# Opening of a gated recurrent and pooling layer: warm-up on a constant, one input piece cast in two parts, two sums held back in the plan

## The chip, the cores and the metric

The kernel runs on one core of a Trainium2 chip. The metric is the device time of one execution in microseconds (us), as the median of several runs. The engines are named as in the profile: PE (TensorE, matmul) with PEld (its weight loads), DVE (VectorE), ACT (ScalarE), POOL (GpSimd) and SP (the engine that issues most DMAs).

## The reference

One layer over 1024 positions of width 1024, in float32, cut to what matters:

```python
h = jnp.einsum('bsd,de->bse', x, w_in[l]) + b_in[l]
xa, za, xb, zb, ga, gb = jnp.split(h, splits, axis=-1)
xa = _causal_depthwise_conv(xa, conv_w[l], conv_b[l])
ya = _rg_lru(xa, w_rgate[l], b_rgate[l], w_igate[l], b_igate[l], lru_lambda[l]) * jax.nn.silu(za)
yb = _multiscale_pool(xb, w_pool[l], b_pool[l], pool_scale[l]) * jax.nn.silu(zb)
merged = (jax.nn.sigmoid(ga) * jnp.einsum('bsw,wd->bsd', ya, w_proj_a[l])
          + jax.nn.sigmoid(gb) * jnp.einsum('bsw,wd->bsd', yb, w_proj_b[l]))
y = jnp.einsum('bsd,de->bse', merged, w_out[l]) + b_out[l]
x = _layer_norm(DEEPNORM_ALPHA * x + y, ln_gain[l], ln_bias[l])
```

The change lies in the first microseconds of the first product, `x @ w_in`. Its 6144 output columns are worked through as 24 groups: `G` groups are the gates `ga` and `gb`, `A` groups the pairs `xa`/`za`, `B` groups the pairs `xb`/`zb`.

## The kernel before, in words

**Products.** A float32 product is made of three matmuls in a narrower float type: each operand is split into a high part (a cast on ACT, names ending in `h`) and a low part (the rest, a subtraction on DVE, names ending in `l`); the products high·high, low·high and high·low are added in PSUM. Each large product is cut into 2x2 blocks and done with seven block products instead of eight, on sums of blocks. One block product is 12 matmuls of 128x512 (four quarters `q` of the contraction, three passes each).

**The input.** `x` arrives transposed as eight raw tiles `xr`, two for each quarter. Its blocks become `x13h/x13l` (two blocks side by side), `x` and `xb` (high and low part in one tile), the differences `t` (made by `sum57`, later `sum6` and `sum4`), and from `t` the tiles `x57h/x57l` and `x64h/x64l`. The first 256 or 512 columns of a tile can be cast by themselves, `PARTS` being the two halves of 512 columns.

**The opening.** `WARM` matmuls on a zeroed tile `warm` run first, into `ps_warm`. Then the first gate group is done without block sums: 96 block passes into `ps_s`, in the order of the quarters, each quarter in the order (kh, h) = (0,0), (1,1), (0,1), (1,0), for both weight blocks `w0h/w0l`. In the first quarter the piece (0,0) is cast and multiplied in two column parts, the others whole.

**What follows.** Group `A0` takes its seven products as `a_A`, `e_A`, `f_A` (product 5), `c_A` (product 7), again `f_A` (product 3); then the next gate group begins with `a_G` and `e_G`, then `a_A` (product 6 of `A0`), `c_G`, `a_G` and so on. Its weights come as raw tiles `ra_G` and `rb_G`; `wah_G/wal_G` is the split of `ra_G`; the split `wd_G` of half of `rb_G` is followed by three block sums in `rb_G` and `ra_G` on DVE, and from these come `wbh_G/wbl_G` (used by `c_G`) and `wch_G/wcl_G` (used by `a_G`). A finished product that is needed later is copied out of PSUM by ACT (`copied`: `m_A<-f_A` is such a copy).

**What sets the order.** The code does not issue instructions: it records them as tasks in a `Plan`. PE and POOL keep the order of the code. For ACT, DVE and SP a list scheduler (`Plan.order`) walks through estimated times, and among the tasks that it takes to be ready it starts the one with the earliest due time; due times are counted back from PE's estimated times. What comes out is written once, in a fixed order for each engine: on the chip each engine works through its list strictly, and an instruction whose input is late holds up everything behind it. All recorded instructions have one line in the profile, the `emit` helper's L388, so they are told apart by tile names.

Of the kernel before, what the change touches and what calls it, by code (L numbers as in the profile page):

```python
# [11 lines left out]
F32 = mybir.dt.float32  # L12
F32R = mybir.dt.float32r
# [3 lines left out]
P = 128  # L17
# [3 lines left out]
H = 512  # L21
# [2 lines left out]
EPS = 1e-5  # L24
WINDOWS = (2, 4, 8, 16)
PAD = 16
WARM = 6
NW = 10
NR = 4
NWORK = 10  # L30
# [24 lines left out]
class Ref:  # L55


    def __init__(self, tile_, v, chain=()):
        self.tile, self.v, self.chain = tile_, v, chain
# [96 lines left out]

class Task:
    __slots__ = ("i", "eng", "op", "args", "kw", "outs", "ins", "deps", "users", "time", "wait", "table", "due",
                 "start", "end", "left", "ready", "chain", "dma", "new", "late")


class Plan:
# [4 lines left out]

    def __init__(self, tc):
        self.tc, self.tasks, self.chained, self.last, self.late = tc, [], [set()], {}, LATEST
        for name, eng in (("tensor", "PE"), ("vector", "DVE"), ("scalar", "ACT"), ("gpsimd", "POOL"), ("sync", "SP")):  # L170
            setattr(self, name, Engine(self, name, eng))

    @contextmanager
    def within(self, us):
        self.late, late = us, self.late
        yield
        self.late = late

    def add(self, name, eng, op, args, kw):
        t = Task()  # L180
        t.late = self.late
        t.i, t.eng, t.op, t.args, t.kw = len(self.tasks), eng, (name, op), args, kw
        refs = [a for a in list(args) + list(kw.values()) if isinstance(a, Ref)]
        out = args[0]
        t.outs = [out] if isinstance(out, Ref) else []
        t.ins = refs[1:] if t.outs else refs
        if isinstance(kw.get("accum_out"), Ref):
            t.ins = [r for r in t.ins if r is not kw["accum_out"]]
            t.outs.append(kw["accum_out"])
        t.deps, t.users, t.new = set(), [], []  # L190
        add = kw.get("accum_op") is not None or (op == "matmul" and not kw.get("start"))
        for refs, write in ((t.ins, False), (t.outs, True)):
            for r in refs:
                s = r.tile
                if t.i not in s.users[-1:]:
                    s.users.append(t.i)
                a0, a1, b = g = r.region()
                for old in ((s.writes, s.reads) if write else (s.writes,)):
                    for (c0, c1, d), j in old:
                        if j != t.i and c0 <= a1 and a0 <= c1 and d & b:  # L200
                            t.deps.add(j)
                if write:

                    for old in (s.writes, s.reads):
                        old[:] = [x for x in old if not (a0 <= x[0][0] and x[0][1] <= a1 and x[0][2] & b == x[0][2])]
                (s.writes if write else s.reads).append((g, t.i))
                if write and s.tag and not s.pool.dram:
                    t.new.append(s)
        t.chain = self.last.get(eng) if eng in ("PE", "POOL") or any(eng in c for c in self.chained) else None
        self.last[eng] = t.i  # L210
        self.cost(t, add)
        self.tasks.append(t)

    def cost(self, t, add):

        name, op = t.op
# [35 lines left out]
    def order(self):  # L252
# [15 lines left out]
                t.due = min(t.due, T[u].due - t.wait)  # L268
        tags = {}
        for t in T:  # L270
            t.left, t.ready, t.start = len(t.deps), 0.0, None
            for s in t.new:
                if s.left == 0:
                    s.left = len(s.users)
                    tags.setdefault(s.tag, ([0.0] * s.pool.bufs, []))[1].append(s)
# [51 lines left out]
        while done < len(T):  # L327
            moved = True
            while moved:
                moved = False  # L330
                while state["pe"] < len(pe) and pe[state["pe"]].left == 0:
                    t = pe[state["pe"]]
# [7 lines left out]
                for e in ("ACT", "DVE", "SP", "POOL"):  # L340
# [17 lines left out]
                    for t in sorted(can, key=key):  # L358
                        end = now + t.time + (1.29 if t.table and state["table"] not in t.table else 0.0)
# [41 lines left out]
def layer_kernel(ctx: ExitStack, tc: tile.TileContext, xq, x, w_in, par, wg, w_pool, wpa, wpb, w_out, rows, out):  # L401
    nc = Plan(tc)
# [24 lines left out]
    def kt(name, dt=F32):  # L427
        return kpool.tile([P, S], dt, tag="k", name=name)

    def et(name):  # L430
        return epool.tile([P, H], F32, tag="e", name=name)

    def bank(name):
        return psum.tile([P, H], F32, tag="ps", name=name)
# [6 lines left out]
    V, A = nc.vector, nc.scalar  # L441
# [171 lines left out]
    def load_group(i, w=None, todo=("12", "4", "75", "63")):  # L613
        w = w or weights_steps(i)
        for js in ("4", "75", "63 apart", "12") if i >= len(order) - 2 else todo:
            w.step(js)
        return w.out
# [332 lines left out]


    begin = ctx.enter_context(ExitStack())
    pass
    warm = kt("warm", F32R)[:, :H]
    V.memset(warm.bitcast(F32), 0.0)
    psw = bank("ps_warm")
    for i in range(WARM):
        nc.tensor.matmul(psw, warm[:, 0:P], warm, start=True, stop=True)
# [16 lines left out]
    def split_w0(n, a, b, h=slice(0, 2)):  # L975
        split(*(w0_part(t, n, a, b)[:, h] for t in (wr, wh, wl)))
# [13 lines left out]
    def split_x(q, kh, h, sl=slice(0, H)):  # L990
        i, p = raws[kh, h]
        split(xr[q][i][:, HALF[p]][:, sl], *(t[:, sl] for t in quarter(q, kh, h)))
# [3 lines left out]
    def mm0(q, kh, h, n, cs=slice(0, H)):  # L996
        sl = slice(q * P, (q + 1) * P)
        passes(ps0[n][h][:, cs], (wh[n][:, kh, sl], wl[n][:, kh, sl]), tuple(t[:, cs] for t in quarter(q, kh, h)),
               q == 0 and kh == h and cs.start == 0, q == KQ - 1 and kh != h)


    PARTS = [slice(0, H // 2), slice(H // 2, H)]
# [63 lines left out]
    def parts(q, n=0):  # L1066
        r = xr[q][0].rearrange("p (i s) -> p i s", i=2)
        todo = [(r, *x13[q])] + [(xr[q][raws[p][0]][:, HALF[raws[p][1]]], *quarter(q, *p)) for p in ((0, 1), (1, 0))]
        for raw, t, u in todo[n:]:
            hi(raw, t)  # L1070
        for raw, t, u in todo[n:]:
            lo(raw, t, u)
        for kh, h in ((0, 0), (1, 1), (0, 1), (1, 0)):
            for n in range(2):
                mm0(q, kh, h, n)

    def each(f, qs, *a):
        for q in qs:
            f(q, *a)

    split_w0(0, 0, 1, slice(0, 1))
    for kh, h in ((0, 0), (1, 1), (0, 1), (1, 0)):
        if kh == h == 1:
            split_w0(0, 0, 1, slice(1, 2))
        for sl in PARTS if kh == h == 0 else (slice(0, H),):
            split_x(0, kh, h, sl)
            mm0(0, kh, h, 0, sl)
        if kh == h == 1:
            split_w0(1, 0, 1)
            mm0(0, 0, 0, 1)  # L1090
        if kh or h:
            mm0(0, kh, h, 1)
# [5 lines left out]
    parts(1, 1)  # L1098
    w = weights_steps(1)
    lower, upper = (0, 1), (2, 3)  # L1100
    each(sum57, lower)
    parts(2)
    each(hi57, lower)
    each(lo57, lower)
# [60 lines left out]

    FILLS = {3: 2, 4: 3, 9: 0, 10: 1}
    for i in range(1, len(order)):
        kind, c = order[i]
        if i in FILLS:
            fill_bias(FILLS[i])  # L1170
        if i == 1:
            W[2] = load_group(2, w_next, ("4", "75", "63"))
        elif i + 1 < len(order):
            W[i + 1] = load_group(i + 1)
# [182 lines left out]
    for i, (n, j) in enumerate(steps):  # L1357
# [10 lines left out]
        for g in range(KQ):  # L1368
# [5 lines left out]
            for q in range(KQ):  # L1374
                sl = slice(q * P, (q + 1) * P)
# [10 lines left out]
            if (n, j) in DONE:  # L1386
                d, h = DONE[n, j]
                d += g
                if j == 3:
                    t, u = ps, et(f"c12_{n}{g}") if n == "b" else None  # L1390
                else:
                    t = u = m1[g] if j == 2 else um[g][:, HALF[h]]
# [193 lines left out]
```

## Time and profile before

| | |
|---|---|
| three runs | 739.67, 740.07, 740.52 us, median 740.07 |
| the profiled execution, its own time | 740.07 us |
| its span, first to last instruction | 738.3 us |
| PE busy | 729.5 us, 99% of the span, 3249 matmuls |
| DVE busy | 600.8 us, 81% |
| ACT busy | 459.0 us, 62% |
| mean granted TensorE clock | 0.998 |

The profiled execution lies on the median; 1.8 us of its time are outside the span. A busy PE here means that a matmul is in flight: matmuls overlap, so the rate is read from the distance between the starts of two of them, not from the duration of one. A row of the timeline gives start, duration, engine, line, operation, output<-inputs and shape; in brackets stands the idle time of that engine before it and what ended it. Equal instructions in a row are merged (x2, x12).

### The profile page before, as it was taken

How to read it: one execution, taken by the hardware profiler on the slowest of the kernel's cores; microseconds unless marked ns; L12 is line 12 of the kernel's file. 1: busy time of each engine (PE TensorE's matmuls, PEld its weight loads, DVE VectorE, ACT ScalarE, POOL GpSimd, SP SyncE). 2: the span in 40 equal slices, each digit the busy share in tenths (PEclk: the TensorE clock that was granted, in tenths of full speed). 3: DMA queues.
4: the chain of work that ended last, by engine and by line, in shares of the span. 5: the costliest groups of instructions: out<-in, count | busy, mean ns of one | idle time of the engine just before them, and what ended most of it. 6: DMA issues, size and time to landing. Idle time of an engine off the chain costs nothing.

```text
span 738.3 us, 8785 instructions
## 1 busy us (share of the span) xinstructions
PE 729.5 (99%) x3249; PEld 599.4 (81%) x3249; DVE 600.8 (81%) x741; ACT 459.0 (62%) x587; POOL 67.9 (9%) x119
## 2 busy tenths in 40 slices
PE   9999999999999999999999999999999999999996
PEld 7887888888787878788888888888888888888885
DVE  7999796969696878977986768879948786999686
ACT  7686959686877868688844445447553545315473
POOL 0171011111101111100011100100000000000021
PEclk9999999999999999999999999999999999999999
DMA  9247979588988989842187954999679996758748
GB/s 320 111 142 198 264 180 279 135 240 224 303 161 217 328 206 282 219 113 91 54 204 154 212 114 158 278 315 331 235 241 303 311 333 234 267 201 232 196 80 149
DMA packets 64227, 158.98 MB, mean 215 GB/s; under 512 B 4340, under 2 KB 8308, under 8 KB 64120
## 3 DMA queue, kind: packets, MB, share of 16 engines
q1 hardware_dynamic: 43512, 106.26, 41.4%
q0 software_dynamic: 20112, 51.91, 33.6%
q8 instruction: 25, 0.41, 0.2%
q10 hardware_dynamic: 560, 0.26, 0.1%
q14 instruction: 18, 0.15, 0.1%
HBM read 137.43 MB, written 77.07 MB: 291 GB/s over the span
## 4 chain that ended last, share of the span: by engine, by line
PE 99%; DVE 1%; DVEq 0%; issue 0%
PE a_A L388 11%; PE a_B L388 11%; PE a_G L388 11%; PE oa L388 6%; PE pa_a L388 6%; PE pa_b L388 6%; PE c_B L388 6%; PE c_A L388 6%; PE c_G L388 5%; PE ps_s L388 3%; PE oc L388 3%; PE pc_b L388 3%; PE pc_a L388 3%; PE ps_pool L388 3%; PE e_B L388 3%; PE e_A L388 3%
## 5 line engine op out<-in xcount | busy, mean ns | idle before, releaser
L388 ACT ACT_TABLE_LOAD x38 | 48.8, 1283 | 3.0 <-issue 2.3
L388 DVE TENSOR_TENSOR i<-i,xc 128x1024 f32<-128x1024 f32 x8 | 9.8, 1225 | 26.9 <-ACT i L388 26.9
L388 DVE SCALAR_TENSOR_TENSOR xc<-xp,par_sb,xc 128x1023 f32<-128x1023 f32 (+2 forms) x24 | 30.7, 1281 | 0.5
L388 PE MATMUL pa_a<-oh,oh 128*128 128x512 f32 x64 | 24.9, 389 | 0.0
L388 PE MATMUL pa_a<-ol,oh 128*128 128x512 f32 x64 | 24.9, 389 | 0.0
L388 PE MATMUL pa_a<-oh,ol 128*128 128x512 f32 x64 | 24.9, 389 | 0.0
L388 PE MATMUL pa_b<-oh,oh 128*128 128x512 f32 x64 | 24.9, 389 | 0.0
L388 PE MATMUL pa_b<-ol,oh 128*128 128x512 f32 x64 | 24.9, 389 | 0.0
L388 PE MATMUL pa_b<-oh,ol 128*128 128x512 f32 x64 | 24.9, 389 | 0.0
L388 ACT ACTIVATE zb<-zb,par_sb 128x1024 f32<-128x1024 f32 (+1 forms) x16 | 15.0, 938 | 14.2 <-DVE zb L388 14.1
L388 ACT ACTIVATE r<-ps_g,par_sb 64x512 f32<-64x512 f32 x32 | 21.9, 683 | 2.1 <-DVE rb_B L388 0.8
L388 ACT ACTIVATE i<-ps_g,par_sb 64x512 f32<-64x512 f32 x32 | 21.9, 684 | 1.9 <-DVE r L388 1.4
L388 PE MATMUL c_A<-x64h,wd_A 128*128 128x512 f32 x64 | 21.0, 389 | 0.0
L388 PE MATMUL c_B<-x64h,wd_B 128*128 128x512 f32 x64 | 21.0, 389 | 0.0
L388 POOL DMA_DIRECT2D out<-y x7 | 8.5, 1210 | 130.0 <-ACT sd L388 117.4
L388 PE MATMUL ps_pool<-mixh,wp 128*128 128x512 f32 x64 | 20.3, 389 | 0.0
L388 PE MATMUL e_A<-x,wah_A 128*128 128x512 f32 x64 | 19.7, 389 | 0.0
L388 PE MATMUL e_B<-x,wah_B 128*128 128x512 f32 x64 | 19.7, 389 | 0.0
L388 POOL COPY paced<-pace 128x1 f32<-128x1 f32 x17 | 6.4, 376 | 130.9 <-ACT pace L388 130.9
L388 PE MATMUL c_G<-x64h,wd_G 128*128 128x512 f32 x56 | 18.4, 389 | 0.0
L388 DVE TENSOR_TENSOR_SCAN r<-a,i 128x1024 f32<-128x1024 f32 x8 | 18.3, 2284 | 0.1
L388 PE MATMUL e_G<-x,wah_G 128*128 128x512 f32 x56 | 17.2, 389 | 0.0
(521 smaller groups left out, 2534.5 us busy)
## 6 DMA issues: line engine op xcount, KB each, us to landing
sg<-sg SPq DMA_DIRECT2D x16, 512.0 KB, 4.3
ra_A<-in_w_in SPq DMA_DIRECT2D x8, 512.0 KB, 7.1
rb_A<-in_w_in SPq DMA_DIRECT2D x8, 512.0 KB, 7.5
xb<-bias SPq DMA_DIRECT2D x4, 1024.0 KB, 12.8
ya<-r SPq DMA_DIRECT2D x8, 512.0 KB, 5.7
xb<-in_x POOLq DMA_DIRECT2D x4, 1024.0 KB, 8.8
ra_B<-in_w_in SPq DMA_DIRECT2D x8, 512.0 KB, 4.3
rb_B<-in_w_in SPq DMA_DIRECT2D x8, 512.0 KB, 6.6
```

The lines of the kernel that those rows point to most:

```text
L388: getattr(getattr(nc, t.op[0]), t.op[1])(*a, **k)
```

## The change

It has three parts. The warm-up reads a constant zero, one column of 128 partitions that is read 512 times over, in place of a tile that DVE zeroes first, and there are eight warm-up matmuls in place of six. The piece (1,1) of the first quarter is cast and multiplied in two parts of 256 columns. And the tasks of `sum57` for the quarters 0 and 1 may not start before 9.0 us of the planner's estimated time.

```diff
-WARM = 6
+WARM = 8
+OPENED = 9.0
...
+    @contextmanager
+    def not_until(self, us):
+        self.early, early = us, self.early
+        yield
+        self.early = early
+
     def add(self, name, eng, op, args, kw):
         t = Task()
-        t.late = self.late
+        t.late, t.early = self.late, self.early
...
-            t.left, t.ready, t.start = len(t.deps), 0.0, None
+            t.left, t.ready, t.start = len(t.deps), t.early, None
...
-    warm = kt("warm", F32R)[:, :H]
-    V.memset(warm.bitcast(F32), 0.0)
+    warm = tc.nc.const_aps.tensor(0.0, [P, H]).bitcast(F32R)
     psw = bank("ps_warm")
     for i in range(WARM):
         nc.tensor.matmul(psw, warm[:, 0:P], warm, start=True, stop=True)
...
-        for sl in PARTS if kh == h == 0 else (slice(0, H),):
+        for sl in PARTS if kh == h else (slice(0, H),):
             split_x(0, kh, h, sl)
             mm0(0, kh, h, 0, sl)
...
-    each(sum57, lower)
+    with nc.not_until(OPENED):
+        each(sum57, lower)
```

Since the planner works on estimated times, the three edits also move other instructions. On PE there are three matmuls more in `ps_s` (six of 256 columns for three of 512) and two more in the warm-up, and nothing else differs. POOL's list is unchanged. On ACT, DVE and SP some instructions change places, at several spots in the first 75 us and at scattered ones later; the three spots that follow are those that the prediction speaks of. Line L388 is L396 in the changed file.

On DVE, in the first quarter (`t_0` is the difference of quarter 0, `xb` and `x_0` are low parts of its pieces), before:

```order
L388 TENSOR_TENSOR x13l_147<-xr_0_89,x13h_142 128x512
L388 TENSOR_TENSOR w0l_172<-w0r_106,w0h_165 128x2x128
L388 TENSOR_TENSOR t_0_175<-xr_0_89,xr_1_95 128x1024
L388 TENSOR_TENSOR xb_170<-xr_1_95,xb_170 128x512
L388 TENSOR_TENSOR x_0_180<-xr_1_95,x_0_180 128x512
L388 TENSOR_TENSOR x13l_201<-xr_0_99,x13h_195 128x512
```

and now:

```order
L396 TENSOR_TENSOR x13l_147<-xr_0_89,x13h_142 128x256 x2
L396 TENSOR_TENSOR w0l_176<-w0r_106,w0h_167 128x2x128
L396 TENSOR_TENSOR xb_173<-xr_1_95,xb_173 128x512
L396 TENSOR_TENSOR x_0_185<-xr_1_95,x_0_185 128x512
L396 TENSOR_TENSOR x13l_206<-xr_0_100,x13h_200 128x512
```

The low part of the second piece is made in two halves, and `t_0` has gone five rows down, behind the first low parts of quarter 1.

On ACT, at the end of product `f_A` (`wah_G` is the cast of the gate group's weights, `m_A<-f_A` the copy of that product out of PSUM, `m_A<-c_A` the copy of the next), before:

```order
L388 ACT_TABLE_LOAD
L388 ACTIVATE sp_y<-sp_m 128x8
L388 CAST wah_G_401<-ra_G_183 128x1024
L388 COPY m_A_430<-f_A_392 128x512
L388 ACT_TABLE_LOAD
L388 ACTIVATE sg_4_467<-ps_s_0_178,par_sb 128x512
L388 ACTIVATE sg_4_467<-ps_s_1_186,par_sb 128x512
L388 COPY m_A_485<-c_A_427 128x512
L388 ACTIVATE bias_432<-bias_432 1x512
```

and now:

```order
L396 ACT_TABLE_LOAD
L396 ACTIVATE sp_y<-sp_m 128x8
L396 COPY m_A_421<-f_A_393 128x512
L396 CAST wah_G_436<-ra_G_192 128x1024
L396 COPY m_A_462<-c_A_419 128x512
L396 ACT_TABLE_LOAD
L396 ACTIVATE sg_4_492<-ps_s_0_181,par_sb 128x512
L396 ACTIVATE sg_4_492<-ps_s_1_188,par_sb 128x512
L396 ACTIVATE bias_423<-bias_423 1x512
```

The cast `wah_G` and the copy `m_A<-f_A` have changed places, and the copy `m_A<-c_A` has come forward, ahead of the table load.

On DVE, where the gate group's later weights are made (`wbl_G` and `wcl_G` are low parts, `xp` and `z` read finished products), before:

```order
L388 TENSOR_TENSOR wbl_G_575<-rb_G_227,wbh_G_566 128x1024
L388 TENSOR_TENSOR ra_G_183<-ra_G_183 128x512
L388 TENSOR_TENSOR wd_A_534<-rb_A_129,wd_A_534 128x512
L388 TENSOR_TENSOR z_597<-a_A_347,m_A_430 128x512
L388 TENSOR_TENSOR wcl_G_605<-ra_G_183,wch_G_593 128x1024
L388 SCALAR_TENSOR_TENSOR xp_397<-f_A_392,par_sb,u_A_603 128x512
```

and now:

```order
L396 TENSOR_TENSOR wbl_G_590<-rb_G_237,wbh_G_583 128x1024
L396 TENSOR_TENSOR ra_G_192<-ra_G_192 128x512
L396 SCALAR_TENSOR_TENSOR xp_397<-f_A_393,par_sb,u_A_588 128x512
L396 TENSOR_TENSOR z_607<-a_A_348,m_A_421 128x512
L396 TENSOR_TENSOR wcl_G_612<-ra_G_192,wch_G_603 128x1024
L396 TENSOR_TENSOR wd_A_553<-rb_A_129,wd_A_553 128x512
```

`xp` and `wd_A` have changed places around `wcl_G`. Between the last two spots DVE's list holds the same instructions in both: `wal_G` (the low part to `wah_G`), eight half-tile differences `t`, the sum `m_A`, five `x64l`, then `wd_G`, the block sums and `sg`.

More of the change, by code (lines that the diff above doesn't have):

```diff
@@ L158 @@
     __slots__ = ("i", "eng", "op", "args", "kw", "outs", "ins", "deps", "users", "time", "wait", "table", "due",
-                 "start", "end", "left", "ready", "chain", "dma", "new", "late")
+                 "start", "end", "left", "ready", "chain", "dma", "new", "late", "early")
 class Plan:
@@ L169, in __init__ @@
         self.tc, self.tasks, self.chained, self.last, self.late = tc, [], [set()], {}, LATEST
+        self.early = 0.0
         for name, eng in (("tensor", "PE"), ("vector", "DVE"), ("scalar", "ACT"), ("gpsimd", "POOL"), ("sync", "SP")):
@@ L952, in layer_kernel @@
     begin = ctx.enter_context(ExitStack())
-    pass
-    warm = kt("warm", F32R)[:, :H]
-    V.memset(warm.bitcast(F32), 0.0)
+    warm = tc.nc.const_aps.tensor(0.0, [P, H]).bitcast(F32R)
     psw = bank("ps_warm")
```

## The prediction, made before the changed kernel had run

> **What bounds the kernel now.** I read the busy shares first, then the chain that ended last, then PE's waits.
>
> ```profile
> PE 729.5 (99%) x3249; PEld 599.4 (81%) x3249; DVE 600.8 (81%) x741; ACT 459.0 (62%) x587; POOL 67.9 (9%) x119
> PE 99%; DVE 1%; DVEq 0%; issue 0%
> PE ps_warm L388 <- DVE warm L388: 1.4, 1, 1.4
> 28.13 2.72 PE a_A L388 x12
> ```
>
> The third row is PE's whole list of waits: after the warm-up begins PE waits for nothing, to its last matmul. So whatever shortens or interrupts PE's stream changes the end by the same amount, and nothing else does. The last row is one block product in the chain: 2.72 / 12 = 0.227 us from one 512-column matmul to the next at full rate.
>
> Now the opening, from the timeline.
>
> ```profile
> 0.24 0.10 POOL L1578 MEMSET const-float32-0.0<- 128x1 f32 x1 [0.24 <-issue]
> ...
> 0.90 0.48 DVE L388 MEMSET warm<- 128x512 f32 x1 [0.90 <-PEq L1578]
> ...
> 1.44 2.93 PE L388 MATMUL ps_warm<-warm 128*128 128x512 f32 x6 [1.44 <-DVE warm L388]
> ...
> 3.73 0.41 ACT L388 CAST x13h<-xr 128x256 fp32r<-128x256 f32 x1
> 4.04 0.29 ACT L388 CAST w0h<-w0r 128x128 fp32r<-128x128 f32 x1
> 4.17 0.42 DVE L388 TENSOR_TENSOR x13l<-xr,x13h 128x256 fp32r<-128x256 f32 x1 [2.79 <-ACT x13h L388]
> ...
> 4.38 0.58 PE L388 MATMUL ps_s<-x13h,w0h 128*128 128x256 f32 x1
> 4.51 0.28 DVE L388 TENSOR_TENSOR w0l<-w0r,w0h 128x128 fp32r<-128x128 f32 x1
> ...
> 5.08 0.62 ACT L388 CAST x13h<-xr 128x512 fp32r<-128x512 f32 x1 [0.17 <-DMA xr<-in_xq]
> ...
> 5.73 0.69 DVE L388 TENSOR_TENSOR x13l<-xr,x13h 128x512 fp32r<-128x512 f32 x1 [0.36 <-ACT x13h L388]
> ...
> 5.88 0.67 PE L388 MATMUL ps_s<-x13h,w0h 128*128 128x512 f32 x1
> ...
> 6.47 0.79 PE L388 MATMUL ps_s<-x13l,w0h 128*128 128x512 f32 x1
> ...
> 7.49 0.44 PE L388 MATMUL ps_s<-x13h,w0h 128*128 128x512 f32 x1
> 7.77 0.40 PE L388 MATMUL ps_s<-x13l,w0h 128*128 128x512 f32 x1
> ...
> 8.93 0.62 PE L388 MATMUL ps_s<-xb,w0h 128*128 128x512 f32 x2
> ```
>
> ```profile
> L388 PE MATMUL ps_warm<-warm x6: 628/628/797, 1.4 to 3.7; 128*128 128x512 f32 x6
> ```
>
> The first warm-up matmul takes 0.797 - 0.628 = 0.17 us more than the others: that is the load of its weights, which every matmul pays that had to wait. The six start (2.93 - 0.63 - 0.17) / 5 = 0.43 us apart, nearly twice 0.227: PE runs at half rate. It still does so up to 7.49, and the next distance, 0.28, is a mixed one; so full rate begins at about 7.6 us, 6.1 us after the first matmul. Between 5.88 and 6.47 lies a hidden gap: the matmul at 5.88 is through at 6.31, the next one waits for the low part (5.73 + 0.69 = 6.42) and streams from 6.47 + 0.17 = 6.64. So 0.33 us are lost there.
>
> **The change, part by part.**
>
> *Warm-up.* DVE's clearing goes (0.48 us). The constant is written at 0.24, before the barrier that PE has passed by 0.90, so PE starts at about 0.9, where DVE's own list begins (an estimate, 0.2 either way). Eight matmuls end streaming at 0.9 + 0.17 + 8 x 0.43 = 4.51. The first real one waits for `w0h` (4.04 + 0.29 = 4.33) and streams from 4.38 + 0.17 = 4.55 as before. So the two matmuls more fit in front, and cost nothing by themselves; if the constant were read at 0.46 us (2.78 / 6 with load, the worst that the rows allow) they would overrun by 0.2 us, at half rate worth 0.1. That end is kept.
>
> *Two column parts.* Two casts of 256 columns follow each other by 4.04 - 3.73 = 0.31, two subtractions by 4.51 - 4.17 = 0.34. So the first half is cast by 5.08 + 0.41 = 5.49, its low part by 5.95, the second half's by 6.29, and the `w0h` behind the second cast comes 0.1 later, ahead of its need. Three matmuls are added, but each of the six has half the columns. If full rate begins at 7.6 as before: six matmuls from 5.88 at 0.213, with one wait to 6.16, end at 7.23 where three ended at 7.49. These 0.26 us are at half rate and worth 0.26 x 0.227 / 0.43 = 0.14 us. If full rate begins before 5.9, the casts set the pace: streams start at 5.71, 6.16, 6.27, 6.39, 6.51, 6.62, then six at 0.227 from 6.74, and `xb` at about 8.1 in place of 8.93: 0.8 us. Gain 0.14 to 0.8; less 0.1 for the overrun at the low end. I take 0.5, the middle of the two computed ends, because the earlier start and the closed gap both favour an earlier switch and nothing in the rows fixes its moment.
>
> The clock is also what the Trainium skill speaks of (TensorE: Matmul & The Clock Gate, Part 1): PE is released to full rate after one busy window of about 3.4 us, and this window runs freely and does not begin with the kernel, so the switch falls 3.4 to 6.8 us after the first matmul, differently in each run. The 6.1 us here agree with that. By this rule the switch would fall evenly between 4.3 and 7.7 us now, the gain would average 0.6 us, and the sum would be 741.9 us.
>
> *Sums held back.* `t_0` and `t_1` leave DVE's path to `xb` and `x`, and their 1.2 us each return later. The tightest place I find in the first 30 us is the low part of quarter 3:
>
> ```profile
> 20.97 1.22 DVE L388 TENSOR_TENSOR x13l<-xr,x13h 128x1024 fp32r<-128x1024 f32 x1
> ...
> 22.76 0.39 PE L388 MATMUL ps_s<-x13l,w0h 128*128 128x512 f32 x1
> ```
>
> It is there 22.76 - 22.19 = 0.57 ahead. The hold leaves DVE idle for at most one `t`, but the `x57l` of quarter 1, as long, now stands behind this instruction. With PE 0.14 to 0.8 ahead this costs 0 to 0.4; I take 0, since the two shifts cancel.
>
> *The moved cast.* This is the term that decides. Now `wah_G` stands behind the copy `m_A<-f_A`, which waits for PE to finish `f_A`.
>
> ```profile
> 34.04 1.04 ACT L388 CAST wah_G<-ra_G 128x1024 fp32r<-128x1024 f32 x1
> 36.33 0.59 ACT L388 COPY m_A<-f_A 128x512 f32<-128x512 f32 x1 [1.25 <-PE f_A L388]
> ...
> 39.38 0.59 ACT L388 COPY m_A<-c_A 128x512 f32<-128x512 f32 x1
> 39.85 1.14 ACT L388 ACTIVATE bias<-bias 1x512 f32<-1x512 f32 x2
> ...
> 46.97 1.05 ACT L388 CAST wbh_G<-rb_G 128x1024 fp32r<-128x1024 f32 x1 [0.62 <-DVE rb_G L388]
> ```
>
> ```profile
> 35.12 1.24 DVE L388 TENSOR_TENSOR wal_G<-ra_G,wah_G 128x1024 fp32r<-128x1024 f32 x1 [0.41 <-ACT wah_G L388]
> ...
> 44.75 0.68 DVE L388 TENSOR_TENSOR wd_G<-rb_G,wd_G 128x512 fp32r<-128x512 f32 x1
> ...
> 46.19 0.69 DVE L388 TENSOR_TENSOR rb_G<-ra_G,rb_G 128x512 f32<-128x512 f32 x1
> ...
> 48.13 1.22 DVE L388 TENSOR_TENSOR wbl_G<-rb_G,wbh_G 128x1024 fp32r<-128x1024 f32 x1
> 49.26 0.69 DVE L388 TENSOR_TENSOR ra_G<-ra_G 128x512 f32<-128x512 f32 x1
> 49.86 0.68 DVE L388 TENSOR_TENSOR wd_A<-rb_A,wd_A 128x512 fp32r<-128x512 f32 x1
> 50.46 0.68 DVE L388 TENSOR_TENSOR z<-a_A,m_A 128x512 f32<-128x512 f32 x1
> 51.12 1.23 DVE L388 TENSOR_TENSOR wcl_G<-ra_G,wch_G 128x1024 fp32r<-128x1024 f32 x1
> ```
>
> ```profile
> 49.73 0.39 PE L388 MATMUL c_G<-x57h,wbh_G 128*128 128x512 f32 x1
> ...
> 50.19 0.39 PE L388 MATMUL c_G<-x57h,wbl_G 128*128 128x512 f32 x1
> ...
> 52.91 0.39 PE L388 MATMUL a_G<-x64h,wcl_G 128*128 128x512 f32 x1
> ```
>
> On PE's old clock: the copy starts at 36.33, its follower 0.47 later (39.85 - 39.38), so `wah_G` runs 36.80 to 37.84. `wal_G`, whose DVE waits in strict order, starts at 37.88 in place of 35.12: **2.76 us late**. From there to `wd_G` DVE holds the same fifteen instructions without idle time in brackets, so the delay passes on whole. The block sum at 46.19 then ends at 46.88 + 2.76 = 49.64, and ACT casts `wbh_G` from 49.73 to 50.78. PE wants it at 49.73; with 0.05 for the signal (4.33 to 4.38) and 0.17 for the load it streams at 51.00: **1.27 us** of standstill. `wbl_G` runs 50.89 to 52.11, so its matmul streams at 52.33 where 50.19 + 1.27 = 51.46 was due: **0.87**. `wcl_G` now stands behind `ra_G`, `xp` and `z`: 50.89 + 1.13 (`wbl_G`) + 0.60 (`ra_G`) + 0.66 (`z`) + 0.61 (`xp`, an estimate by its neighbours) = 53.89 to 55.12, streamed at 55.34 where 52.91 + 2.14 = 55.05 was due: **0.29**. `wd_A` behind it ends 0.6 later, at about 55.7, and is read only by a product that follows `a_G`. Together 2.43 us. The chain begins with a PE matmul and ends at one, so an earlier PE shifts all of it and recovers none; and as PE had no wait, nothing later absorbs it. Some twenty steps at 0.02 us give 2.0 to 2.8.
>
> *The rest.* `m_A<-c_A` ahead of the table load delays what stands behind it by one copy, 0.59, where DVE is itself 2.76 late. The rearranged SP loads and late ACT and DVE pairs cost nothing that I can see, since PE never waited on any; up to 0.5 if one does.
>
> Sum: 740.07 (the profiled execution, also the median; span 738.3) + 2.43 - 0.5 = **742.0 us**. Ends: +2.8 - 0.04 = 742.8, +2.0 - 0.8 = 741.3.
>
> **The rivals.**
>
> *The delay is hidden* and only the opening counts: 740.07 - 0.5 = 739.6. For it: in the whole run before PE waited for neither engine, so the lists have room. Against it: the room is 52.91 - 52.35 - 0.22 = 0.34 at `wcl_G` and 50.19 - 49.35 - 0.22 = 0.62 at `wbl_G`, and the delay is 2.76. It decides from a delay under 0.34, which means a copy done 2.4 us before `f_A` is. Chance 0.07.
>
> *The delay is half hidden*, only `wbh_G`'s 1.27 being paid, with a gain of 0.6: 740.7. The other two waits follow from the same DVE list, which speaks against it. Chance 0.08.
>
> *Half rate comes back* after the standstills, 2.4 us in 5.6: if it lasts the 6.1 us of the opening, half of that is lost, 742.0 + 3.0 = 745.0. No row shows PE idle in mid-run. The Trainium skill (the same page, Why this matters for your kernels) sees the rate fall only after idle gaps of some 3 us; the longest here would be 1.3, so by it the time stays at 742.0. Chance 0.04.
>
> *Another moved instruction comes late too*: 742.0 + 0.5 to 1 = 742.5 to 743. Chance 0.06.
>
> **Chances.** The forecast keeps 0.75. A measurement can tell about 0.2% here, 1.5 us: slower means over 741.55. The forecast's lower end lies a little under that (0.06 of its 0.75). Slower: 0.69 + 0.04 + 0.06 = 0.79. Same: 0.06 + 0.08 and most of the hidden case, 0.18. Faster: 0.03, a hidden delay with more than the opening that I count. The range 740.7 to 743.0 takes in the half-hidden case and leaves out the hidden one and the half rate.
>
> **What would show it.** Warm-up from about 0.9, the first `ps_s` still near 4.4, `xb` between 8.1 and 8.8. In ACT's list `wah_G` right behind a copy that waited for `f_A`, on DVE some 2 us of idle time before `wal_G`, and in PE's waits new rows for `c_G` (on `wbh_G` and `wbl_G`, 2.1 together) and `a_G` (0.3). The prediction is wrong if PE shows no wait at `c_G`, or if `wah_G` comes before 36 us.

## The result, and the profile after

| | before | changed |
|---|---|---|
| median | 740.29 us (739.67 to 741.12, 8 runs) | 742.49 us (741.97 to 743.77, 8 runs) |
| ratio | | 1.0031, 95% interval 1.0020 to 1.0042 |
| span of the profiled execution | 738.3 us | 740.7 us |

The change makes the kernel 0.31% slower, 1.5 to 3.1 us. The forecast was 742.0 us with a range of 740.7 to 743.0. The busy shares, the shares of the chain, and PE's whole list of waits in the changed kernel (in the waits: time in all, times, longest):

```profile
PE 730.5 (99%) x3254; PEld 599.8 (81%) x3254; DVE 600.9 (81%) x741; ACT 459.4 (62%) x588; POOL 67.2 (9%) x119
PE 96%; DVE 2%; DMA 1%; issue 0%; ACT 0%; ACTq 0%; DVEq 0%
PE c_G L396 <- ACT wbh_G L396: 0.9, 1, 0.9
PE ps_warm L396 <- PEq L1585: 0.8, 1, 0.8
PE c_G L396 <- DVE wbl_G L396: 0.6, 1, 0.6
PE ps_s L396 <- ACT w0h L396: 0.6, 1, 0.6
```

PE is 99% busy in both kernels, so the share says nothing; the list of waits does. Before it held only the start. Now there are two waits at `c_G`, on the two instructions that the forecast named, and one in the opening, on `w0h`, that it did not.

The chain in the middle, of the changed kernel, in order of time (start, length, what):

```profile
33.62 2.73 PE f_A L396 x12
...
36.37 0.03 ACT m_A L396
36.40 0.46 issue
36.86 1.06 ACT wah_G L396
...
37.94 1.23 DVE wal_G L396
...
51.03 1.14 DVE wbl_G L396
...
52.21 2.57 PE c_G L396 x10
```

The path that sets the end leaves PE at the end of `f_A`, goes through the copy `m_A` and the cast `wah_G` on ACT, then through DVE's list (whose timeline rows from `wal_G` to `wbl_G` have no idle time in brackets), and comes back to PE at `c_G` 15.9 us after `f_A` ended. On PE it looks like this:

```profile
49.55 0.39 PE L396 MATMUL a_A<-x64h,wcl_A 128*128 128x512 f32 x1
50.89 0.50 PE L396 MATMUL c_G<-x57h,wbh_G 128*128 128x512 f32 x1 [0.95 <-ACT wbh_G L396]
51.22 0.40 PE L396 MATMUL c_G<-x57l,wbh_G 128*128 128x512 f32 x1
52.21 0.51 PE L396 MATMUL c_G<-x57h,wbl_G 128*128 128x512 f32 x1 [0.60 <-DVE wbl_G L396]
52.56 0.39 PE L396 MATMUL c_G<-x57h,wbh_G 128*128 128x512 f32 x1
52.79 0.40 PE L396 MATMUL c_G<-x57l,wbh_G 128*128 128x512 f32 x1
...
54.85 0.39 PE L396 MATMUL a_G<-x64l,wch_G 128*128 128x512 f32 x1
55.21 0.50 PE L396 MATMUL a_G<-x64h,wcl_G 128*128 128x512 f32 x1
55.55 0.39 PE L396 MATMUL a_G<-x64h,wch_G 128*128 128x512 f32 x1
```

The bracket gives the time in which no matmul was in flight. What counts is the distance of the starts: 50.89 - 49.55 - 0.23 = 1.11, and the matmul that had to wait is followed 0.33 later in place of 0.23, for its late weight load: 1.21 in all. The wait for `wbl_G` costs 0.76 + 0.12 = 0.88 in the same way. The forecast wait at `a_G` is there too, 55.21 - 54.85 - 0.23 = 0.13 and 0.11 behind it, 0.24 in all; the list of waits doesn't show it, because a matmul was still in flight. The whole standstill is read between two matmuls on either side of all three waits, before and in the changed kernel:

```profile
33.41 0.39 PE L388 MATMUL f_A<-x57h,wbh_A 128*128 128x512 f32 x1
...
57.89 0.39 PE L388 MATMUL c_G<-x64h,wd_G 128*128 128x512 f32 x1
```

```profile
33.45 0.39 PE L396 MATMUL f_A<-x57h,wbh_A 128*128 128x512 f32 x1
...
60.35 0.39 PE L396 MATMUL c_G<-x64h,wd_G 128*128 128x512 f32 x1
```

From the first matmul of `f_A` to the first `c_G<-x64h,wd_G` there were 57.89 - 33.41 = 24.48 us before, and now 60.35 - 33.45 = 26.90: **2.42 us of standstill**. The start of `f_A` is level with before (33.45 against 33.41). These two make the span's 2.4 us.

The opening of the changed kernel, from the timeline:

```profile
0.77 3.75 PE L396 MATMUL ps_warm<-const-float32-0.0 128*128 128x512 f32 x8 [0.77 <-PEq L1585]
4.42 0.58 PE L396 MATMUL ps_s<-x13h,w0h 128*128 128x256 f32 x1
...
6.53 0.28 PE L396 MATMUL ps_s<-x13l,w0h 128*128 128x256 f32 x1
...
6.65 0.28 PE L396 MATMUL ps_s<-x13h,w0l 128*128 128x256 f32 x1
7.03 0.40 ACT L396 CAST w0h<-w0r 128x256 fp32r<-128x256 f32 x1 [1.19 <-DMA w0r<-in_w_in]
...
7.49 0.50 PE L396 MATMUL ps_s<-x13h,w0h 128*128 128x512 f32 x1 [0.57 <-ACT w0h L396]
...
8.97 0.61 PE L396 MATMUL ps_s<-xb,w0h 128*128 128x512 f32 x2
```

PE starts at 0.77, goes over to full rate at about 6.2 us (its 256-column matmuls follow each other by 0.22 up to 6.13, then by 0.16, then by 0.12), and starts the last matmul of the piece (1,1) at 6.65. Then it stands still: the next matmuls need the second weight block of quarter 0, whose raw piece `w0r` landed at 7.01. `xb` begins at 8.97, where it began at 8.93 before. All that was won was lost to this landing.

### The profile page after: what moved, and what is told of

Same layout as the page of the kernel before. It is cut to its first block, busy times and chain, and to the rows that moved or that the text cites. A ratio compares the mean times of both kernels' runs of the same rounds, so it can differ in the third digit from the quotient of the medians.

```text
span 740.7 us, 8801 instructions
## 1 busy us (share of the span) xinstructions
PE 730.5 (99%) x3254; PEld 599.8 (81%) x3254; DVE 600.9 (81%) x741; ACT 459.4 (62%) x588; POOL 67.2 (9%) x119
## 4 chain that ended last, share of the span: by engine, by line
PE 96%; DVE 2%; DMA 1%; issue 0%; ACT 0%; ACTq 0%; DVEq 0%
PE a_B L396 11%; PE a_A L396 11%; PE a_G L396 10%; PE oa L396 6%; PE pa_a L396 6%; PE pa_b L396 6%; PE c_B L396 6%; PE c_A L396 6%; PE c_G L396 5%; PE oc L396 3%; PE pc_b L396 3%; PE pc_a L396 3%; PE ps_pool L396 3%; PE e_B L396 3%; PE e_A L396 3%; PE ps_s L396 3%
## 5 line engine op out<-in xcount | busy, mean ns | idle before, releaser
L396 DVE SCALAR_TENSOR_TENSOR xc<-xp,par_sb,xc 128x1023 f32<-128x1023 f32 (+2 forms) x24 | 30.7, 1281 | 0.5
L396 DVE TENSOR_TENSOR i<-i,xc 128x1024 f32<-128x1024 f32 x8 | 9.8, 1224 | 26.2 <-ACT i L396 26.2
L396 PE MATMUL pa_a<-oh,oh 128*128 128x512 f32 x64 | 24.9, 389 | 0.0
L396 PE MATMUL pa_a<-ol,oh 128*128 128x512 f32 x64 | 24.9, 389 | 0.0
L396 PE MATMUL pa_a<-oh,ol 128*128 128x512 f32 x64 | 24.9, 389 | 0.0
L396 PE MATMUL pa_b<-oh,oh 128*128 128x512 f32 x64 | 24.9, 389 | 0.0
L396 PE MATMUL pa_b<-ol,oh 128*128 128x512 f32 x64 | 24.9, 389 | 0.0
L396 PE MATMUL pa_b<-oh,ol 128*128 128x512 f32 x64 | 24.9, 389 | 0.0
L396 ACT ACTIVATE zb<-zb,par_sb 128x1024 f32<-128x1024 f32 (+1 forms) x16 | 15.0, 939 | 14.4 <-DVE zb L396 14.3
L396 ACT ACTIVATE r<-ps_g,par_sb 64x512 f32<-64x512 f32 x32 | 21.9, 684 | 2.1 <-DVE rb_B L396 0.8
L396 ACT ACTIVATE i<-ps_g,par_sb 64x512 f32<-64x512 f32 x32 | 21.9, 684 | 1.9 <-DVE r L396 1.4
L396 PE MATMUL c_A<-x64h,wd_A 128*128 128x512 f32 x64 | 21.0, 389 | 0.0
L396 PE MATMUL c_B<-x64h,wd_B 128*128 128x512 f32 x64 | 21.0, 389 | 0.0
L396 PE MATMUL ps_pool<-mixh,wp 128*128 128x512 f32 x64 | 20.3, 389 | 0.0
L396 POOL DMA_DIRECT2D out<-y x7 | 8.5, 1210 | 129.4 <-ACT sd L396 114.3
L396 PE MATMUL e_A<-x,wah_A 128*128 128x512 f32 x64 | 19.7, 389 | 0.0
L396 PE MATMUL e_B<-x,wah_B 128*128 128x512 f32 x64 | 19.7, 389 | 0.0
L396 PE MATMUL c_G<-x64h,wd_G 128*128 128x512 f32 x56 | 18.4, 389 | 0.0
L396 DVE TENSOR_TENSOR_SCAN r<-a,i 128x1024 f32<-128x1024 f32 x8 | 18.3, 2284 | 0.1
L396 POOL COPY paced<-pace 128x1 f32<-128x1 f32 x17 | 6.8, 401 | 125.0 <-ACT pace L396 125.0
L396 PE MATMUL e_G<-x,wah_G 128*128 128x512 f32 x56 | 17.2, 389 | 0.0
```

The costliest lines, as they stand in the source:

```text
L396: getattr(getattr(nc, t.op[0]), t.op[1])(*a, **k)
```

## The experiments

All changes of code are against the changed kernel. Ratios are to the kernel before, timed on the same chip.

**The hold at 8.0.** The plan is sensitive: with one number changed, the cast is back in its place.

```diff
-OPENED = 9.0
+OPENED = 8.0
```

> The whole change, but the held sums may start from 8.0 us of the plan's time in place of 9.0. The warm-up, the two column parts and PE's list are those of the change; on ACT the cast wah_G stands ahead of the copy m_A<-f_A again, and DVE's list is that of before to xc at 55 us except that t_0 stays two rows later. Theory (the loss is the moved cast, 2.42 us of PE standstill at c_G and a_G): no wait of PE on wbh_G, wbl_G or wcl_G, and 742.5 - 2.4 = 740.1 us, 739.5 to 740.6, level with the kernel before or up to 0.8 us faster. Rival 1 (the loss comes from the opening itself, the late w0r piece and the changed warm-up, and the standstills only show where it ends up): about 741.5 to 742.5, whatever the order on ACT. Rival 2 (the opening gains its 0.5 us once the cast is back): 739.6.

Measured: 740.01 us, ratio 0.9986 (0.9977 to 0.9996). Its whole list of PE waits, and ACT's rows at the cast from its timeline:

```profile
PE ps_s L396 <- ACT w0h L396: 0.8, 1, 0.8
PE ps_warm L396 <- PEq L1585: 0.8, 1, 0.8
```

```profile
34.73 1.03 ACT L396 CAST wah_G<-ra_G 128x1024 fp32r<-128x1024 f32 x1
36.67 0.59 ACT L396 COPY m_A<-f_A 128x512 f32<-128x512 f32 x1 [0.90 <-PE f_A L396]
```

The cast is done 0.9 us before the copy can start, and no wait at `c_G` or `a_G` is left. The loss goes with this order: rival 1 is out. The copy `m_A<-c_A` has also gone back behind the table load here; that the cast is what counts is read from the chain above, where `wal_G` waits for it. No run moved the two apart. The opening still waits for `w0r`, so rival 2's full gain isn't there either.

**The cast pulled forward in another way.**

```diff
-    w_next.step("12")
+    with nc.within(8.0):
+        w_next.step("12")
```

> The whole change, with the step of the plan that splits the gate group's first weights given an earlier due time (within 8 us of the place in the program). wah_G stands ahead of m_A<-f_A again, but now the casts of wd_A and wd_G and three x64h stand behind the copy m_G<-a_G, which waits for PE. A half dose of the same mechanism. Theory: PE waits once at c_G for wbl_G, about 0.8 us, and about 0.3 at a_G, 1.1 us in all in place of 2.42, so 742.5 - 1.3 = 741.2 us (740.7 to 741.6). Rival 1 (only the cast wah_G counts): no wait, 740.1. Rival 2 (loss from the opening): 742 or more.

Measured: 741.24 us, ratio 1.0001 (0.9992 to 1.0010).

One wait of PE is left in mid-run, and ACT's timeline shows why:

```profile
PE c_G L396 <- DVE wbl_G L396: 0.5, 1, 0.5
```

```profile
33.66 1.04 ACT L396 CAST wah_G<-ra_G 128x1024 fp32r<-128x1024 f32 x1
...
43.77 0.59 ACT L396 COPY m_G<-a_G 128x512 f32<-128x512 f32 x1 [0.94 <-ACT x64h L396]
44.25 0.62 ACT L396 CAST wd_A<-rb_A 128x512 fp32r<-128x512 f32 x1
44.77 0.62 ACT L396 CAST wd_G<-rb_G 128x512 fp32r<-128x512 f32 x1
```

The fault has moved to the next copy: `wd_A` and `wd_G` now stand behind `m_G<-a_G`. From `f_A` to `c_G<-x64h,wd_G` it takes 58.23 - 32.64 = 25.59 us, a standstill of 1.11, as expected: half the loss. Timed beside it on the same chip, this run lies 1.23 us above the hold at 8.0 (741.24 against 740.01). Against the kernel before, beside it at 740.95, no loss can be told.

**The warm-up alone.**

```diff
-        for sl in PARTS if kh == h else (slice(0, H),):
+        for sl in PARTS if kh == h == 0 else (slice(0, H),):
-OPENED = 9.0
+OPENED = 0.0
```

> Of the change only the warm-up: constant zero and eight matmuls; one column part and no hold. All lists in the first 60 us as before. Theory: no standstill in mid-run, and only the opening is measured: PE starts at 0.8 in place of 1.4, its full rate comes earlier, but PE then waits for the third w0r piece if that lands at 7.0, so 740.3 - 0.2 = 740.1 (739.7 to 740.4). Rival 1 (the earlier start pays in full): 739.5 to 739.8. Rival 2 (the warm-up on a constant costs something by itself, by eight matmuls that overrun the first operands): 740.6 to 741.

Measured: 740.89 us, ratio 0.9999 (0.9988 to 1.0010). The median alone misses the theory's band and lies in rival 2's, but the kernel before, beside it, had 740.95, so the ratio decides: the constant and the two matmuls more bring nothing and cost nothing that can be told, and rival 1 is out. PE waited for `w0h` (cast from 6.97) and then for `xb`'s low part.

**The hold alone.** Warm-up with six matmuls on the zeroed tile, one column part:

```diff
-WARM = 8
+WARM = 6
-    warm = tc.nc.const_aps.tensor(0.0, [P, H]).bitcast(F32R)
+    warm = kt("warm", F32R)[:, :H]
+    V.memset(warm.bitcast(F32), 0.0)
-        for sl in PARTS if kh == h else (slice(0, H),):
+        for sl in PARTS if kh == h == 0 else (slice(0, H),):
```

> Of the change only the held sums (9.0): six matmuls on the zeroed tile, one column part. The plan moves wah_G behind m_A<-f_A as in the whole change. Theory: the full standstill without any change of the opening, PE waits at c_G and a_G of 2.4 us together, 740.3 + 2.4 = 742.7 us (742.2 to 743.1). Rival 1 (the late cast hurts only together with the other parts): 740.3. Rival 2 (loss from the warm-up or the w0r piece): 740.3.

Measured: 742.80 us, ratio 1.0027 (1.0016 to 1.0037).

Its two rows of waits at `c_G`:

```profile
PE c_G L396 <- ACT wbh_G L396: 0.9, 1, 0.9
PE c_G L396 <- DVE wbl_G L396: 0.6, 1, 0.6
```

The same standstill, 60.12 - 33.25 - 24.48 = 2.39 us, with the old warm-up and the piece cast whole as before. It is the plan's order, not the opening, that costs.

**The change without the hold** (`OPENED = 0.0`).

> The change without the hold: warm-up on the constant with eight matmuls and two column parts; the sums may start at once. ACT's and SP's lists are those of the change, DVE's differs in two rows of the opening. Theory (wah_G behind the copy is all that counts, and the two parts alone move it too): waits at c_G and a_G of 2.4 us as in the change, 742.5 us (741.9 to 743.0), within 0.3 of the change run beside it. Rival 1 (the held sums are what moves the cast): no waits, 740.1. Rival 2 (t_0 ahead of xb on DVE costs the opening): 742.7 to 743.3.

Measured: 742.81 us, ratio 1.0031 (1.0021 to 1.0042), standstill 59.88 - 33.00 - 24.48 = 2.40. The two column parts, beside a warm-up that by itself brings no standstill, push the cast behind the copy as well. So either of two edits does it, and the hold at 9.0 adds nothing; at 8.0 it undoes it. DVE's rows in quarter 0:

```profile
7.46 0.69 DVE L396 TENSOR_TENSOR xb<-xr,xb 128x512 fp32r<-128x512 f32 x1
8.07 1.22 DVE L396 TENSOR_TENSOR t<-xr,xr 128x1024 f32<-128x1024 f32 x1
```

`t_0` (the row `t`) stands behind `xb` here too, though nothing holds it: the two parts move it there. So rival 2's condition was not met, and this run says nothing on it.

**The change once more, and the kernel before once more.**

> The change itself once more, as a control beside the others and for a second profile of its opening. Theory: 742.5 us (742.0 to 743.0); the standstill at c_G and a_G again 2.4 us, since all times in it are those of instructions; the opening differs by up to 1 us with the landing of the third w0r piece (5.5 to 7.2) and with the moment at which full rate begins (4.9 to 7.6 so far). Rival (the first profile's opening is the change's own, and not chance): the piece lands at 7.0 again and xb begins at 9.0.

> The kernel before once more, for a second profile of its opening. Theory (the early landing of the third w0r piece, by 5.6 us, was chance in the first profile): it lands later, 6.0 to 7.2, xb begins at 8.9 or later, and PE shows a wait or a late start in quarter 0 there; 740.0 to 741.2 us. Rival (the landing belongs to each kernel's order): 5.6 again.

Measured: the change 742.91 us, ratio 1.0030 (1.0020 to 1.0040), standstill 60.78 - 33.91 - 24.48 = 2.39, `w0h` cast from 7.48. The kernel before, one run of 740.99 us:

```profile
7.31 0.40 ACT L388 CAST w0h<-w0r 128x256 fp32r<-128x256 f32 x1 [1.54 <-DMA w0r<-in_w_in]
...
7.75 0.43 DVE L388 TENSOR_TENSOR w0l<-w0r,w0h 128x256 fp32r<-128x256 f32 x1 [1.25 <-ACT w0h L388]
...
8.09 1.22 DVE L388 TENSOR_TENSOR t<-xr,xr 128x1024 f32<-128x1024 f32 x1
...
9.23 0.68 DVE L388 TENSOR_TENSOR xb<-xr,xb 128x512 fp32r<-128x512 f32 x1
...
9.27 0.39 PE L388 MATMUL ps_s<-xb,w0h 128*128 128x512 f32 x1
...
9.97 0.50 PE L388 MATMUL ps_s<-xb,w0h 128*128 128x512 f32 x1 [0.31 <-DVE xb L388]
```

In the first profile of before that cast began at 5.60; here it begins at 7.31. The early landing was chance. And here it is seen what the new order on DVE, with `t_0` behind `xb`, is good for: in the old one DVE, itself late for the missing `w0r`, makes `t_0` before `xb`'s low part, and PE waits (9.97 - 9.27 - 0.23 = 0.47, and 0.11 for the load behind it).

**The late piece issued elsewhere.** Both on top of the hold at 8.0, with every other order kept; the piece is taken out of ACT's list after the plan is made.

```diff
     dma_w0(1, 0, 1)
+    piece = nc.tasks[-1]
     dma_x(0, 0, HALF[1])
+    nc.requeue = piece, nc.tasks[-1]
...
         order = self.order()
+        piece, after = self.requeue
+        piece.op = ("sync", "dma_start")
+        order.remove(piece)
+        order.insert(order.index(after) + 1, piece)
```

> As the run with the hold at 8.0, and the DMA of the third w0r piece (the second weight block of quarter 0, wanted by PE at about 6.8) goes to SP's queue, behind the third x piece, where ACT's queue issued it; all other orders are the same. In the profiles so far that piece was there between 5.5 and 7.2 us, and PE waited for it in three of six. Theory (the opening's gain is eaten by this landing): the piece is there before 6.3, PE has no wait on w0h after its first matmul, xb begins near 8.2 in place of 9.0, and 740.0 - 0.5 = 739.5 us (739.0 to 739.8). Rival 1 (the DMA engines are full, so the two xr pieces behind it come later by as much, and PE waits for xb or its low part): 740.0, 739.8 to 740.4. Rival 2 (the landing is not what holds the opening): 740.0 with xb near 9.

Measured: 740.50 us, ratio 0.9996 (0.9987 to 1.0005). `w0h` is cast from 6.19, PE has no wait at quarter 0 and `xb` begins at 8.36, as the theory had it; but `xb`'s low part comes 0.18 late and a matmul on `w0l` at 17.5 another 0.41, and `f_A` begins 25.24 after `xb` where it was 24.48 in the change. These two make 0.59 of the 0.76 between the two distances. The time went as rival 1 says, if only in part where it says; 740.50 is well over the theory's band and 0.1 over rival 1's. The ratio is no better than with ACT's queue.

With `("gpsimd", "dma_start")` and position 0 in its place:

> As the run with the hold at 8.0, with the third w0r piece issued by POOL as its first instruction, on a queue of its own, where ACT's queue issued it third. On SP's queue that piece was there at 6.2, but the x pieces behind it came later and 0.75 us were given back by 28 us. Theory (the DMA engines are shared, so a piece that comes earlier takes the time from another): the piece is there before 6.5 and xb begins by 8.5, but a_A begins no earlier than 27.6, and the time is 739.7 to 740.5, no better than with the hold at 8.0 by more than 0.3. Rival (a queue of its own costs the others nothing): a_A at 27.2 and 739.2 to 739.6.

Measured: 740.23 us, ratio 0.9991 (0.9982 to 0.9999).

```profile
1.30 0.90 POOL L400 DMA_DIRECT2D w0r<-in_w_in  x1 [0.86 <-POOLq L1590]
...
5.56 0.71 ACT L400 CAST x13h<-xr 128x256 fp32r<-128x256 f32 x2 [0.63 <-DMA xr<-in_xq]
6.18 0.40 ACT L400 CAST w0h<-w0r 128x256 fp32r<-128x256 f32 x1
...
8.55 0.62 PE L400 MATMUL ps_s<-xb,w0h 128*128 128x512 f32 x2
```

PE has no wait left but the start, and the span is 738.1 us, the shortest of these profiles; but the `x` piece ahead of it in ACT's list is cast 0.43 later than in the change (5.56 against 5.13, and 5.10 where the piece lay on SP's queue). `a_A` begins at 27.59, where the theory had it (27.6; the rival 27.2), and over the next kernel, timed beside it, no lead can be told.

**The hold at 8.0 once more,** beside the last one.

> The change with the hold at 8.0 once more, beside the version before it and for a second profile. Theory: no wait at c_G and a_G; the opening set by the landing of the third w0r piece plus 1.95 us to xb, wherever in 5.6 to 7.5 it falls; 740.0 us (739.6 to 740.5), 0.1 to 0.2% under the kernel before. Rival (its lead over the kernel before was chance): a ratio of 1.000 or above.

Measured: 740.24 us, ratio 0.9994 (0.9983 to 1.0004), no wait in mid-run; `w0h` cast from 7.66, `xb` at 9.61. Against the first time (0.9986) the two intervals overlap; a lead over the kernel before of about 0.1% is likely, and the second interval alone doesn't show it.

All profiles side by side. The standstill is the time from `f_A` to `c_G<-x64h,wd_G` less 24.48:

| profile | `w0h` cast from | `xb` | `f_A` | `f_A` less cast | standstill |
|---|---|---|---|---|---|
| before | 5.60 | 8.93 | 33.41 | 27.81 | 0 |
| before again | 7.31 | 9.27 | 34.35 | 27.04 | 0 |
| warm-up alone | 6.97 | 8.92 | 34.02 | 27.05 | 0 |
| hold alone | 6.79 | 8.75 | 33.25 | 26.46 | 2.39 |
| change | 7.03 | 8.97 | 33.45 | 26.42 | 2.42 |
| change again | 7.48 | 9.43 | 33.91 | 26.43 | 2.39 |
| without hold | 6.49 | 8.44 | 33.00 | 26.51 | 2.40 |
| hold at 8.0 | 7.19 | 9.14 | 33.75 | 26.56 | 0.01 |
| hold at 8.0 again | 7.66 | 9.61 | 34.23 | 26.57 | 0 |
| cast pulled | 6.08 | 8.16 | 32.64 | 26.56 | 1.11 |
| piece on SP | 6.19 | 8.36 | 33.60 | 27.41 | 0.05 |
| piece on POOL | 6.18 | 8.55 | 33.03 | 26.85 | 0 |

Where the piece comes late, by ACT's queue, `xb` begins 1.95 us after the cast, whatever the warm-up and the parts; `f_A` follows after 27.05 where `t_0` stands ahead of `xb` on DVE, and after 26.42 to 26.57 where it stands behind. That is the 0.5 to 0.6 us that the change really wins in the opening, and it goes with DVE's order, not with PE's rate: both of these profiles with `t_0` ahead show PE waiting for `xb` (0.3 in their lists), and no other list has this wait. The hold alone brings this order (26.46) and the two column parts without the hold bring it as well (26.51), so the gain belongs to neither edit by itself.

## Why the prediction was right, and where it was not

*The moved cast:* right, step by step. `wal_G` was forecast for 37.88 and began at 37.94, after 1.98 us of idle time on DVE; the standstill was worked out as 1.27 + 0.87 + 0.29 = 2.43 and measured 2.42, of which the three places show 1.21, 0.88 and 0.24 and the remaining 0.09 is not assigned to a matmul. The forecast took 0.17 for a late weight load, from the half-rate warm-up; here it cost 0.10 to 0.12. So the agreement to 0.01 is partly luck, the one to 0.1 is not. The hold at 8.0 takes all of it away, the cast pulled forward half, the hold alone brings it back; so it is shown, not only read off.

*The warm-up:* right in its parts (start at 0.77 for 0.9, first real matmul at 4.42 for 4.4, no cost of the two matmuls more), without effect on the time.

*Two column parts:* this step failed. For an early full rate the six matmuls were to start at up to 6.62, and they did (6.65); but the sum went straight on to `xb` at 8.1, and `xb` came at 8.97, outside the 8.1 to 8.8 that were named as a sign. It had the cast of the next weight block `w0h` only 0.1 later than before and "ahead of its need", and so took the raw piece for landed; the profile before happened to show the piece there in time, and in every other profile the piece came 0.5 to 2.1 us later. The gain of 0.5 us became -0.04 in the profile. That is the 0.5 us between 742.0 and 742.49. Against its own base the miss is smaller: a loss of 1.93 was forecast, and the medians show 742.49 - 740.29 = 2.20.

*Sums held back:* costed at nothing, with an eye only on what might come late. In fact the order that they make on DVE has a gain, of 0.5 to 0.6 us, in executions in which the piece is late, though the column parts make it without the hold too; the first profile of before showed no such wait, and so it couldn't be seen there. By the medians the change costs 2.2, which fits the 2.42 less a part of this gain; how often the piece is late was not measured.

*The rest:* nothing else came late; from `c_G<-x64h,wd_G` to the end nothing was lost.

*The rivals.* The delay was not hidden, nor half hidden. Half rate did not come back: after the standstills the matmuls follow each other by 0.23 (52.56 to 52.79). The Trainium skill (TensorE: Matmul & The Clock Gate, Why this matters for your kernels) has only idle gaps of some 3 us bring it back; with gaps of 1.11 and 0.76 us the trace agrees, and no run here has one of 3 us.

*The clock.* Its moment moves from run to run: full rate began from about 4.9 us (hold at 8.0) to 7.6 us (before), 4.1 to 6.1 us after the first matmul. That lies within 3.4 to 6.8 us, an estimate from the free-running window of 3.4 us in the Trainium skill (the same page, Part 1). The time worked out from it, 741.9, fell short by 0.6 where mine fell short by 0.5, for the same reason: soon after the rate rose, PE had nothing to multiply (from the matmul at 6.65 to the one at 7.49).

## What to carry to other kernels

Where a planner writes one strict list for each engine, look first in the difference of the orders for an instruction that has slipped behind one that waits for the engine that bounds the kernel; the delay is then passed on down the next engine's list, and here it could be worked out to 0.1 us from the profile before. A gain in an opening is worth only what the next operand's landing allows: follow each matmul to its DMA before counting it, and don't trust one profile for a landing. A plan that changes its order at a small edit should be tried with its constant shifted: 8.0 in place of 9.0 took away the whole standstill of 2.4 us here.

## What the runs showed of the hardware

One and the same DMA, 128 KB, third on ACT's queue and issued at 1.67 in the change, was there between 5.6 at the latest and 7.66 us in different executions, while the first `x` pieces on SP's queue were cast from 3.7 to 3.8 in each of them. The rows of the DMA queues up to 9 us, with the piece on POOL's queue:

```profile
q10 hardware_dynamic: 288, 0.13, 5.3%
q0 software_dynamic: 48, 0.13, 4.4%
```

By ACT's queue (q10) all three pieces made 560 packets, so this one 272; by POOL's (q0) it made 48, and it was there by 6.18. Whether the small packets are the cause of the late landing was not tried apart from the queue.
